# Modulation vectors of a diffusion trunk: from VectorE sums to TensorE matmuls with a narrow stationary operand

## The chip, the cores and the metric

One core of a Trainium2 chip runs the whole program. The metric is the device time of one execution in microseconds (us); the figure for a kernel is the median over its runs. TensorE is called PE here, VectorE DVE, ScalarE ACT, GpSimd POOL and SyncE SP; SP issues nearly all DMAs.

## The reference

Two trunk layers work on 640 tokens (512 latent, 128 context) of width 1024, all in float32. Each layer first makes six modulation vectors of length 1024 from a conditioning vector, and uses them around its mixer and its MLP:

```
mod = silu(cond) @ mod_w[li] + mod_b[li]              # 1024 -> 6 x 1024
sh1, sc1, g1, sh2, sc2, g2 = split(mod, 6)
h = rmsnorm(x, norm_mix_pre[li]) * (1 + sc1) + sh1
y = even_mixer(h, ...) if li == 0 else odd_mixer(h, ...)
x = x + g1 * rmsnorm(y, norm_mix_post[li])
h = rmsnorm(x, norm_mlp_pre[li]) * (1 + sc2) + sh2
x = x + g2 * rmsnorm(relu(h @ mlp_w1[li])**2 @ mlp_w2[li], norm_mlp_post[li])
```

There are two conditioning vectors: `c` for the latent tokens, `c_ctx` for the context tokens. So each modulation matrix (1024 x 6144, 25 MB a layer) is multiplied with two vectors only. Layer 0's mixer is a short gated convolution beside differential attention, layer 1's is neighbourhood attention beside windowed attention.

## The kernel before, in words

**Stages.** `run` opens five phases in turn: `first` (constants, norm and the first weights of layer 0), `mix0` (layer 0's mixer), `wide` (its output projection and MLP), `mix1`, and `wide` again for layer 1. In the trace they begin at about 0, 65, 360, 890 and 1200 us; MLP 0 is the part from about 404 to 890, MLP 1 from about 1254.

**Large matmuls.** They run in float32r with both operands split into a high and a low part, three matmuls per product (`gemm_tok` L232 to L234, `gemm_feat` L243 to L245). Weights come as `raw` tiles (three buffers) by DMA on the SP queue, ACT casts the high part and DVE or POOL subtracts the low one (`unit`, L213 to L218). Results go to PSUM buffers that `mm` hands out: two in the mixers; in a `wide` phase it goes round two `mm` buffers, `po` and, in most of the MLP, four `tp` buffers. In the MLP a block of 1024 hidden features is made in two halves, each by eight `gemm_feat` groups whose relu is L487, and then added to the output by ten `gemm_tok` tiles (L501, L503).

**The first two vectors of layer 0** (shift and scale of the mixer) are summed by PE in stage `first` (`mod_quarter`): the stationary operand is `silu32`, 128 x 32, in which two columns hold silu(c) and silu(c_ctx) and the others are zero. Four matmuls go to the four groups of 32 array columns and write the four 32-partition strips of one PSUM tile (L317); DVE copies it (L320), and two small matmuls with a selection matrix turn the sums into columns (L323).

**The other ten vectors** are summed by DVE, in half vectors of 512 (`mod_slab`): four DMAs of 512 KB from `mod_w` into `mraw` (L339), and for each of eight chunks of 128 rows and each of the two conditions one DVE product with a per-partition scalar, added up in `acc` (L295, L297). Later `mod_sum` splits `acc` into high and low parts (ACT L348; L349 on DVE for layer 0, on POOL for layer 1), sums over the partitions with four PE matmuls with `pick`, a stationary operand of two columns (L352), and copies the row `gr` (L356). Shifts and scales go through DRAM to be laid out as columns (`crow`, `mc`) and end in the tables A and B (`mod_dest`); gates get bias and gain and go to DRAM as rows (`grow`), from which `load_gates` broadcasts them.

**Where this work stands.** `background` takes one half vector from a list. Layer 0's vectors 2, 4 and 3 are called for in `mixer0` and its convolution (six half vectors), layer 0's 5 and layer 1's 1, 2 and 0 in blocks 1 and 2 of MLP 0 (eight), layer 1's 4, 3 and 5 in `mixer1` (six).

**Order.** No order is written out. A planner places every instruction on its engine's queue by priority, which is program order, and by its own estimate of when operands and buffers are ready. `high_priority(-300)` puts what is issued under it 300 places later than it stands, so `background` work yields to the work around it. The queues of the engines, and SP's queue of DMAs, are then run strictly in the planned order. `weave` interleaves two generators, attention steps (`main`) and projection tiles (`fill`).

Of the kernel before, what the change touches and what calls it, by code (L numbers as in the profile page):

```python
# [38 lines left out]
class Trunk:  # L39
    def __init__(self, ctx, tc, I, O):  # L40
        self.tc, self.nc, self.I, self.O = tc, tc.nc, I, O
        pool = lambda name, **k: ctx.enter_context(tc.tile_pool(name=name, **k))
        self.const = pool("const", bufs=1)
        self.stats = pool("stats", bufs=10)
        self.small = pool("small", bufs=8)
        self.wpool = pool("w", bufs=1)
        self.s10 = pool("s10", bufs=10)
        self.shared = pool("shared", bufs=1)
        self.ps = pool("ps", bufs=1, space=PSUM)
        self.dram = pool("scratch", bufs=1, space=DRAM)  # L50
        self.n = self.turn = self.deep = 0
        self.begun = []
# [6 lines left out]
    def slot(self, name, dt=F32, c=640):  # L59
# [7 lines left out]
        "mix0": ({"ln": (1024, 3), "ck0": (512, 1), "v0": (768, 2), "e": (640, 4), "pT": (640, 3), "cb": (642, 1), "yd": (640, 2)}, {"big": (1024, 2)}),  # L67
# [48 lines left out]
    def constants(self):  # L116
# [3 lines left out]
        pick = self.tk("pick", 4)  # L120
        nc.vector.memset(pick, 0.0)
        nc.vector.memset(pick[:, 0:4:3], 1.0)
        self.pick = c.tile([P, 2, 2], F32R, name="pick")
        nc.scalar.copy(self.pick.rearrange("p a b -> p (a b)"), pick)
# [25 lines left out]
        self.silu32 = self.tk("silu32", 256, tag="t2").rearrange("p (k c) -> p k c", k=KC)  # L150
# [19 lines left out]
        self.crow = self.dram.tile([2, 2, 1024], F32, name="crow")  # L170
# [76 lines left out]
    def background(self, jobs, n=1):  # L247

        for job in self.begun:
            job()  # L250
        self.begun = []
# [5 lines left out]
    def weave(self, main, n_main, fill, n_fill):  # L257
# [30 lines left out]

    def mod_acc(self, acc, w, kc, first):

        nc = self.nc
        for c in range(2):
            s = self.silu[:, kc, c:c + 1]
            if first:
                nc.vector.tensor_scalar(acc[:, c, :], w, s, None, ALU.mult)  # L295
            else:
                nc.vector.scalar_tensor_tensor(acc[:, c, :], w, s, acc[:, c, :], ALU.mult, ALU.add)  # L297
# [34 lines left out]
    def mod_slab(self, li, vec, half):  # L332
        nc = self.nc
        mw = self.I["mod_w"][li]
        c0 = vec * 1024 + half * 512
        acc = self.tk("acc").rearrange("p (c n) -> p c n", c=2)
        for u in range(4):
            r = self.tk("mraw").rearrange("p (k n) -> p k n", k=2)
            nc.sync.dma_start(r, mw[u * 256:(u + 1) * 256, c0:c0 + 512].rearrange("(k p) n -> p k n", p=P))  # L339
            for j in range(2):  # L340
                self.mod_acc(acc, r[:, j, :], 2 * u + j, u + j == 0)
        return lambda: self.mod_sum(li, vec, half, acc)

    def mod_sum(self, li, vec, half, acc):

        nc = self.nc
        hl = self.wpool.tile([P, 2, 2, 512], F32R, tag="hl", bufs=4, name=self.nm("hl"))
        nc.scalar.copy(hl[:, 0], acc)  # L348
        (nc.gpsimd if li else nc.vector).tensor_tensor(hl[:, 1], acc, hl[:, 0].bitcast(F32), ALU.subtract)  # L349
        p = self.mm()[:2]  # L350
        for i in range(4):
            nc.tensor.matmul(p, self.pick[:, i % 2, :], hl[:, i // 2, i % 2, :], start=i == 0, stop=i == 3)  # L352
        row = self.tk("gr", 512, tag="t2")[:2]
        w = vec // 3
        if vec % 3 < 2:
            nc.vector.tensor_copy(row, p)  # L356
            d = self.crow[vec % 2, :, half * 512:half * 512 + 512]
            nc.sync.dma_start(d, row)
            cols = self.stats.tile([P, 4, 2], F32, tag="mc", bufs=2, name=self.nm("mc"))
            for c in range(2):  # L360
                nc.sync.dma_start(cols[:, :, c], d[c].rearrange("(k p) -> p k", p=P))
            return self.mod_dest(li, vec, half * 4, cols.rearrange("p k c -> p (k c)"))
        r0 = li * 48 + vec * 8 + half * 4
        bias, gain = (self.tk("gr", 512, tag="t2")[:2] for _ in range(2))
        nc.sync.dma_start(bias, self.I["modb"][r0:r0 + 4, :].rearrange("(o k) n -> o (k n)", o=1).to_broadcast([2, 512]))
        r0 = 61 + (2 * li + w) * 8 + half * 4
        nc.sync.dma_start(gain, self.I["vecs"][r0:r0 + 4, :].rearrange("(o k) n -> o (k n)", o=1).to_broadcast([2, 512]))
        nc.vector.tensor_tensor(row, p, bias, ALU.add)
        nc.vector.scalar_tensor_tensor(row, row, ROOT, gain, ALU.mult, ALU.mult)
        gi = (li * 2 + w) * 2  # L370
        nc.sync.dma_start(self.grow[gi:gi + 2, half * 512:half * 512 + 512], row)
# [101 lines left out]
    def mlp(self, li, H, jobs, after):  # L473
# [3 lines left out]
        for b in range(4):  # L477
            F = self.new_h("f")
            for s in range(2):
                self.deep = DEEP if b < 3 and b + s else 0  # L480
                units = self.slab(I["mlp_w1"][li], 0, ((b * 1024 + s * 512, 512),), lo="dve" if b or s else "pool")
                for c0, n in GROUPS:
                    for m in range(4):
                        p = self.mm()
                        self.gemm_feat(units, m, rhs(0, c0, n), rhs(1, c0, n), p[:, :n])
                        q = self.tk("r", 384, tag="t3")[:, :n]
                        nc.scalar.activation(q, p[:, :n], AF.Relu)  # L487
                        hi = F[0][s][:, m, c0:c0 + n]
# [3 lines left out]
                if b:  # L492
                    self.background(jobs)
            for n in range(2):
                units = self.slab(I["mlp_w2"][li], b * 1024, ((n * 512, 512),))
                for t in range(NT):
                    p = self.mm()
                    ap = lambda part: (lambda kc: F[part][kc // 4][:, kc % 4, t * P:(t + 1) * P])
                    self.gemm_tok(units, ap(0), ap(1), p)
                    if b == 0:  # L500
                        nc.scalar.copy(Y[n][:, t, :], p)  # L501
                    else:
                        nc.vector.tensor_tensor(Y[n][:, t, :], Y[n][:, t, :], p, ALU.add)  # L503
                    if b == 3 and n == 1:
                        after(Y, ss, G, t)
                if b == 3 and n == 0:
                    G = self.load_gates(li * 2 + 1)
                    ss = [self.gate_first(Y[0], t, G) for t in range(NT)]
                elif 0 < b < 3:
                    self.background(jobs)  # L510
            if b == 3:
                assert not jobs and not self.begun
# [169 lines left out]
    def mixer0(self, H, jobs):  # L682
# [4 lines left out]
        for h in range(4):  # L687
            fill, n = (chain(self.qkv_head(H, h + 1, heads), conv), 5) if h < 3 else (conv, 0)
            n += CONV_STEPS[h]
            self.weave(self.diff_attn(heads[h], yB), 6, fill, n)  # L690
            if h < 3:
                self.background(jobs)
# [3 lines left out]
    def conv_branch(self, H, jobs, out):  # L696
# [6 lines left out]
        for which, half in ((2, 0), (2, 1), (1, 0), (1, 1), (0, 0), (0, 1)):  # L703
            self.background(jobs, half)
# [95 lines left out]
    def mixer1(self, H, jobs):  # L800
# [54 lines left out]
        def q_tiles():  # L855
            self.background(jobs)
# [15 lines left out]
        def v_tiles():  # L872
            self.background(jobs)
# [37 lines left out]
        def qk_groups(hc):  # L911
            self.background(jobs)
# [168 lines left out]
    def run(self):  # L1081
        jobs = lambda li, vecs: [lambda v=v, h=h: self.mod_slab(li, v, h) for v in vecs for h in range(2)]
# [3 lines left out]
        todo = jobs(0, (2, 4, 3))  # L1086
# [8 lines left out]
        with self.phase("wide"):  # L1095
            H = self.rest(0, y, Y0, todo, jobs(0, (5,)) + jobs(1, (1, 2, 0)))
            todo = jobs(1, (4, 3, 5))
        with self.phase("mix1"):
            y, Y0 = self.mixer1(H, todo)
        with self.phase("wide"):  # L1100
            self.rest(1, y, Y0, todo, [])

    def rest(self, li, y, Y0, todo, jobs):
# [9 lines left out]
        while todo or self.begun:  # L1113
            self.background(todo)
# [99 lines left out]
```

## Time and profile before

| | |
|---|---|
| Median of 3 runs | 1722.18 us (1720.81 to 1725.09) |
| The profiled execution | 1719.25 us; its span, first to last instruction, 1717.4 us |
| Mean granted PE clock | 0.974 of 2.4 GHz |
| PE busy | 1623.5 us, 95% of the span |
| PE weight loads | 1418.3 us, 83% |
| DVE busy | 926.8 us, 54% |
| ACT busy | 665.9 us, 39% |
| POOL busy | 304.3 us, 18% |
| HBM read | 172.93 MB, 109 GB/s in the mean |

The busy share of PE is modelled from pipelined instructions that overlap, so the distance from the start of one matmul to the next says more than the length of one. The granted clock is the mean of two levels, 1.2 and 2.4 GHz: 0.5 in a stretch is all of it at the lower one. A float32 matmul (not float32r) appears as two records.

### The profile page before, as it was taken

The numbers are of one execution on the slowest core, as the hardware profiler recorded it, in microseconds if no ns is written. First come the engines' busy times: TensorE is split into PE (matmuls) and PEld (weight loads), VectorE is DVE, ScalarE is ACT, GpSimd is POOL, SyncE is SP. The second block draws the span as 40 slices with busy tenths as digits, with TensorE's granted clock in tenths as the row PEclk, the third lists the DMA queues.
The fourth block names the chain that finished last, engine by engine and source line by source line (L and its number), as shares of the span: only waits on it lengthen the run. The fifth ranks groups of instructions, "written<-read, shape, count | busy, mean of one in ns | idle before, by whom it ended". The sixth has DMA issues, their size and how long they took to land. (4 is left out here: it accounts for less than half of the span.)

```text
span 1717.4 us, 23382 instructions
## 1 busy us (share of the span) xinstructions
PE 1623.5 (95%) x9088; PEld 1418.3 (83%) x9088; DVE 926.8 (54%) x1539; ACT 665.9 (39%) x1389; POOL 304.3 (18%) x339
## 2 busy tenths in 40 slices
PE   6889998987999999899997899999989999999998
PEld 4878787876989988789886678898789898898996
DVE  3386768637732758754367845743564143342433
ACT  4543443435333313223344645445464242141331
POOL 1342343134000001100144300431330000000002
PEclk9979898999999999999999999999999999999999
DMA  9334314235431434433144214421453131222222
GB/s 298 88 102 123 89 59 122 93 123 173 150 110 50 147 124 142 153 100 122 56 140 149 93 58 134 130 83 53 151 172 99 50 98 54 94 62 86 77 71 86
DMA packets 140015, 187.38 MB, mean 109 GB/s; under 512 B 32499, under 2 KB 71728, under 8 KB 139904
## 3 DMA queue, kind: packets, MB, share of 16 engines
q1 hardware_dynamic: 139904, 185.89, 34.3%
q8 instruction: 71, 1.16, 0.3%
q14 instruction: 40, 0.33, 0.1%
HBM read 172.93 MB, written 14.50 MB: 109 GB/s over the span
## 5 line engine op out<-in xcount | busy, mean ns | idle before, releaser
L297 DVE SCALAR_TENSOR_TENSOR acc<-mraw,silu,acc 128x512 f32<-128x512 f32 x280 | 216.0, 814 | 62.8 <-DMA mraw<-mod_w 62.5
L216 ACT CAST hl<-raw 128x1024 fp32r<-128x1024 f32 (+2 forms) x184 | 169.7, 930 | 181.9 <-DMA raw<-mlp_w 53.4
L218 DVE TENSOR_TENSOR hl<-raw,hl 128x1024 fp32r<-128x1024 f32 (+2 forms) x138 | 161.0, 1181 | 116.3 <-ACT hl L216 115.2
L243 PE MATMUL mm<-hhi,hl 128*128 128x384 f32 (+1 forms) x652 | 208.6, 321 | 7.8 <-DVE gr L356 5.5
L245 PE MATMUL mm<-hhi,hl 128*128 128x384 f32 (+1 forms) x652 | 205.2, 316 | 1.7 <-DVE hl L218 1.6
L244 PE MATMUL mm<-hlo,hl 128*128 128x384 f32 (+1 forms) x652 | 205.0, 315 | 0.8 <-DVE hlo L406 0.8
L490 DVE TENSOR_TENSOR r<-r 128x256 f32<-128x256 f32 (+1 forms) x128 | 62.0, 488 | 147.8 <-ACT fhi L489 147.7
L243 PEld LDWEIGHTS mm<-hhi,hl 128*128 128x128 f32 x652 | 125.6, 193 | 11.6 <-DVE gr L356 6.4
L245 PEld LDWEIGHTS mm<-hhi,hl 128*128 128x128 f32 x652 | 125.1, 192 | 3.2 <-DVE hl L218 1.9
L244 PEld LDWEIGHTS mm<-hlo,hl 128*128 128x128 f32 x652 | 125.7, 193 | 1.5 <-DVE hlo L406 1.1
L441 POOL TENSOR_TENSOR yacc<-yacc,G 128x512 f32<-128x512 f32 x20 | 28.8, 1453 | 519.0 <-ACT junk L385 501.1
L349 POOL TENSOR_TENSOR hl<-acc,hl 128x1024 fp32r<-128x1024 f32 x12 | 31.9, 2661 | 481.5 <-ACT hl L348 481.5
L233 PE MATMUL tp<-hl,fhi 128*128 128x512 f32 x262 | 104.3, 399 | 5.0 <-DVE hl L218 5.0
L234 PE MATMUL tp<-hl,flo 128*128 128x512 f32 x262 | 103.8, 397 | 0.0
L232 PE MATMUL tp<-hl,fhi 128*128 128x512 f32 x262 | 102.6, 398 | 0.0
L218 POOL TENSOR_TENSOR hl<-raw,hl 128x512 fp32r<-128x512 f32 (+1 forms) x46 | 85.4, 1868 | 66.0 <-ACT hl L216 55.0
L232 PE MATMUL mm<-hl,hhi 128*128 128x384 f32 (+2 forms) x232 | 85.4, 371 | 6.6 <-DVE rb L556 4.6
L234 PE MATMUL mm<-hl,hlo 128*128 128x384 f32 (+2 forms) x232 | 84.0, 363 | 3.2 <-DVE hlo L406 3.2
L243 PE MATMUL tp<-hhi,hl 128*128 128x384 f32 (+1 forms) x276 | 86.3, 314 | 0.0
L244 PE MATMUL tp<-hlo,hl 128*128 128x384 f32 (+1 forms) x276 | 86.3, 314 | 0.0
L233 PE MATMUL mm<-hl,hhi 128*128 128x384 f32 (+2 forms) x232 | 84.4, 364 | 1.6 <-POOL hl L218 1.6
L245 PE MATMUL tp<-hhi,hl 128*128 128x384 f32 (+1 forms) x276 | 85.2, 313 | 0.0
(425 smaller groups left out, 3934.6 us busy)
## 6 DMA issues: line engine op xcount, KB each, us to landing
raw<-mlp_w SPq DMA_DIRECT2D x128, 512.0 KB
mraw<-mod_w SPq DMA_DIRECT2D x80, 512.0 KB
mw<-mod_w SPq DMA_DIRECT2D x8, 1024.0 KB
raw<-w_out SPq DMA_DIRECT2D x16, 512.0 KB
xs<-x SPq DMA_DIRECT2D x15, 512.0 KB
x<-xs SPq DMA_DIRECT2D x15, 512.0 KB
raw<-w_in_even SPq DMA_DIRECT2D x48, 128.0 KB
raw<-w_in_even SPq DMA_DIRECT2D x24, 256.0 KB
```

Of the source, the lines that this page charges most:

```text
L216: nc.scalar.copy(hi, raw)
L218: eng.tensor_tensor(hl[:, 1, :, :width], raw, hi.bitcast(F32), ALU.subtract)
L232: nc.tensor.matmul(out, lhi(kc), hi, start=kc == 0, stop=False)
L233: nc.tensor.matmul(out, lhi(kc), lo, start=False, stop=False)
L234: nc.tensor.matmul(out, llo(kc), hi, start=False, stop=kc == nk - 1)
L243: nc.tensor.matmul(out, hi, rhi(kc), start=kc == 0, stop=False)
L244: nc.tensor.matmul(out, hi, rlo(kc), start=False, stop=False)
L245: nc.tensor.matmul(out, lo, rhi(kc), start=False, stop=kc == KC - 1)
L297: nc.vector.scalar_tensor_tensor(acc[:, c, :], w, s, acc[:, c, :], ALU.mult, ALU.add)
L349: (nc.gpsimd if li else nc.vector).tensor_tensor(hl[:, 1], acc, hl[:, 0].bitcast(F32), ALU.subtract)
L441: self.nc.gpsimd.tensor_tensor(Y0[:, t, :], Y0[:, t, :], G[0 if t < NS else 1][:, 0:512], ALU.mult)
L490: nc.vector.tensor_tensor(q, q, q, ALU.mult)
```

## The change

All ten remaining vectors are now summed by PE, as `mod_quarter` does for the first two. `mod_steps` is a generator; one step takes n chunks of 128 rows of one vector (n = 1 in layer 0's mixer, 2 in the MLPs): it asks for the float32 weights of this step and the next (tiles of 128 x 1024, 512 KB each), multiplies each chunk in four matmuls, one for each group of 32 array columns, with `silu32` as the stationary operand and 256 weight columns streamed, and DVE copies or adds the 128 x 256 result into `mrow`. After the eighth chunk `mod_finish` turns the sums into columns with two small matmuls and finishes them there: shifts and scales without DRAM, gates by a scattered write to `grow`. `mod_acc`, `mod_slab`, `mod_sum`, `pick` and `crow` go.

The calls move too: in mixer 0 `weave` makes one call after each of the 24 attention steps (three vectors, eight steps each); in the MLPs there is a call after every four `gemm_feat` groups and after token tiles 1 and 4. Layer 1's vectors 1, 0, 2, 4 and 3 are all made in MLP 0, after layer 0's 5 (24 steps), and layer 1's 5 at the start of MLP 1 (four steps); mixer 1 has none. The tag `ln`, which holds the weights, gets four buffers instead of three in the wide phases.

```diff
-        "wide": ({"ln": (1024, 3), "G": (1024, 2), "hx": (2048, 1), "t3": (512, 6)}, {"tp": (512, 4)}),
+        "wide": ({"ln": (1024, 4), "mrow": (256, 2), "G": (1024, 2), "hx": (2048, 1), "t3": (512, 6)}, {"tp": (512, 4)}),
...
     def background(self, jobs, n=1):
-        for job in self.begun:
-            job()
-        self.begun = []
         for _ in range(n):
-            if jobs:
-                with self.tc.high_priority(-300):
-                    self.begun.append(jobs.pop(0)())
+            with self.tc.high_priority(-300):
+                next(jobs, None)
...
             next(main)
+            self.background(jobs)
...
+    def mod_steps(self, vecs, n, ahead):
+        nc = self.nc
+        steps = [(li, vec, k) for li, vec in vecs for k in range(0, KC, n)]
+        tiles = {}
+        for i, (li, vec, k) in enumerate(steps):
+            for j in range(i, min(i + ahead + 1, len(steps))):
+                if j not in tiles:
+                    l, v, k0 = steps[j]
+                    tiles[j] = [self.tk("mraw") for _ in range(n)]
+                    for m, w in enumerate(tiles[j]):
+                        r0 = (k0 + m) * P
+                        nc.sync.dma_start(w, self.I["mod_w"][l][r0:r0 + P, v * 1024:v * 1024 + 1024])
+            p = self.mm()[:, :256]
+            for m, w in enumerate(tiles[i]):
+                w = w.rearrange("p (h g n) -> p h g n", h=2, g=4)
+                for g in range(4):
+                    nc.tensor.matmul(p[32 * g:32 * g + 32].rearrange("p (h n) -> p h n", h=2), self.silu32[:, k + m, :],
+                                     w[:, :, g, :], start=m == 0, stop=m == n - 1)
+            if k == 0:
+                rows = self.tk("mrow", 256)
+                nc.vector.tensor_copy(rows, p)
+            else:
+                nc.vector.tensor_tensor(rows, rows, p, ALU.add)
+            if k + n == KC:
+                self.mod_finish(li, vec, rows)
+            yield
+
+    def mod_finish(self, li, vec, rows):
+        nc = self.nc
+        q = self.mm()[:, :16]
+        pick = self.ident.rearrange("p (g r) -> p g r", r=32)[:, :, 0:2]
+        for h in range(2):
+            nc.tensor.matmul(q[:, 8 * h:8 * h + 8].rearrange("p (g c) -> p g c", c=2), rows[:, h * P:(h + 1) * P], pick,
+                             start=h == 0, stop=True, skip_group_check=True)
+        if vec % 3 < 2:
+            return self.mod_dest(li, vec, 0, q)
...
+        nc.vector.tensor_tensor(gate, q.rearrange("p (k c) -> p c k", c=2), b, ALU.add)
+        g = self.npost(li, w).unsqueeze(1).to_broadcast([P, 2, 8])
+        nc.vector.tensor_tensor(gate, gate, g, ALU.mult)
+        for c in range(2):
+            nc.sync.dma_start(self.grow[(li * 2 + w) * 2 + c, :].rearrange("(k p) -> p k", p=P), gate[:, c, :])
...
-        todo = jobs(0, (2, 4, 3))
+        todo = self.mod_steps([(0, 2), (0, 4), (0, 3)], 1, 1)
...
-            H = self.rest(0, y, Y0, todo, jobs(0, (5,)) + jobs(1, (1, 2, 0)))
-            todo = jobs(1, (4, 3, 5))
+            H = self.rest(0, y, Y0, todo, self.mod_steps([(0, 5), (1, 1), (1, 0), (1, 2), (1, 4), (1, 3)], 2, 1))
...
-            self.rest(1, y, Y0, todo, [])
+            self.rest(1, y, Y0, iter(()), self.mod_steps([(1, 5)], 2, 1))
```

## Rows read from the trace of the kernel before

**Rows 1.** By stretch: PE, PEld, DVE, ACT, POOL busy, PE clock, DMA, GB/s:
```profile
80.00:350.00 270.00, 251.37 (x1368) 215.98 (x1367) 198.69 (x343) 114.27 (x280) 85.73 (x95) 0.92 0.32 95
...
880.00:960.00 80.00, 64.96 (x344) 53.34 (x342) 63.12 (x99) 38.31 (x89) 41.20 (x47) 0.93 0.43 139
...
1290.00:1690.00 400.00, 400.00 (x2223) 362.42 (x2222) 143.79 (x201) 123.99 (x195) 6.45 (x5) 1.00 0.23 74
```

**Rows 2.** The same stretches, instructions that touch the tile acc alone:
```profile
80.00:350.00 270.00, 0.00 (x0) 0.00 (x0) 84.74 (x102) 6.29 (x6) 0.00 (x0) 0.92 0.32 95
...
880.00:960.00 80.00, 0.00 (x0) 0.00 (x0) 21.38 (x28) 1.05 (x1) 2.40 (x1) 0.93 0.43 139
```

**Rows 3.** One line's instructions: ns min/median/max, first and last start; relus, picks:
```profile
L487 ACT ACTIVATE r<-mm x12: 364/385/493, 418.3 to 588.1; 128x256 f32<-128x256 f32 x7, 128x384 f32<-128x384 f32 x5
...
L487 ACT ACTIVATE r<-mm x16: 366/491/493, 588.1 to 830.2; 128x384 f32<-128x384 f32 x10, 128x256 f32<-128x256 f32 x6
...
L487 ACT ACTIVATE r<-po x7: 365/387/492, 1266.8 to 1431.9; 128x256 f32<-128x256 f32 x4, 128x384 f32<-128x384 f32 x3
...
L487 ACT ACTIVATE r<-po x9: 383/387/492, 1431.9 to 1654.9; 128x256 f32<-128x256 f32 x5, 128x384 f32<-128x384 f32 x4
...
L352 PE MATMUL mm<-hl,pick x20: 386/394/402, 587.9 to 801.8; 128*2 128x512 f32 x20
```

**Rows 4.** What PE waited for: us in total, times, longest:
```profile
PE mm L243 <- DVE gr L356: 5.5, 2, 4.5
...
PE tp L233 <- DVE hl L218: 5.0, 1, 5.0
...
PE mm L232 <- DVE rb L556: 4.6, 1, 4.6
...
PE s L1061 <- DVE nx L968: 4.2, 3, 3.5
...
PE pt L564 <- DVE e L765: 3.7, 3, 1.8
```

**Rows 5.** Short stretches, columns as in Rows 1:
```profile
85.00:112.00 27.00, 21.41 (x76) 16.15 (x76) 24.99 (x37) 10.54 (x27) 15.51 (x18) 0.63 0.35 110
...
177.00:198.00 21.00, 18.78 (x76) 14.24 (x76) 16.48 (x24) 8.45 (x18) 11.15 (x12) 0.76 0.40 121
...
286.00:294.00 8.00, 6.55 (x28) 6.55 (x29) 8.00 (x15) 0.62 (x1) 6.36 (x4) 0.57 0.54 144
...
928.00:935.00 7.00, 4.63 (x11) 3.70 (x12) 6.84 (x11) 0.00 (x0) 1.66 (x1) 0.52 0.50 151
```

**Rows 6.** PE in order of time, stage first: start us, us, records:
```profile
39.82 1.52 PE L317 MATMUL pt<-mw,silu 128*32 128x256 f32 x12
...
41.27 0.44 PE L676 MATMUL mm<-hl,hhi 128*128 128x384 f32 x1
...
46.57 0.34 PE L678 MATMUL mm<-hl,hlo 128*128 128x384 f32 x1
...
46.74 0.51 PE L678 MATMUL acc<-hl,hlo 128*128 128x384 f32 x2
...
47.18 1.93 PE L317 MATMUL pt<-mw,silu 128*32 128x256 f32 x32
```

**Rows 7.** PE in order of time, the small matmuls of stage first:
```profile
21.90 0.58 PE L323 MATMUL tp<-sel,mr 128*128 128x4 f32 x4 [0.62 <-DVE mr L320]
```

**Rows 8.** PE in order of time, one set of pick matmuls:
```profile
706.83 1.09 PE L352 MATMUL tp<-hl,pick 128*2 128x512 f32 x4
```

**Rows 9.** Two lines of stage first, columns as in Rows 3:
```profile
L317 PE MATMUL pt<-mw,silu x128: 376/380/637, 15.9 to 48.7; 128*32 128x256 f32 x128
...
L320 DVE COPY mr<-pt x4: 418/425/425, 21.3 to 49.2; 128x256 f32<-128x256 f32 x4
```

**Rows 10.** What DVE waited for, columns as in Rows 4:
```profile
DVE acc L297 <- DMA mraw<-mod_w: 62.5, 39, 4.0
```

**Rows 11.** DVE by line, 85 to 112 us: busy us, mean ns, idle before:
```profile
L297 DVE SCALAR_TENSOR_TENSOR acc<-mraw,silu,acc 128x512 f32<-128x512 f32 x16 | 13.4, 886 | 1.0 <-DMA mraw<-mod_w 1.0
```

More of the change, by code (lines that the diff above doesn't have):

```diff
@@ L66 @@
         "first": ({"x0": (1024, 1), "junk": (512, 3), "mw": (2048, 4), "mr": (256, 2), "ab": (8, 8)}, {"acc": (512, 2), "tp": (512, 2)}),
-        "mix0": ({"ln": (1024, 3), "ck0": (512, 1), "v0": (768, 2), "e": (640, 4), "pT": (640, 3), "cb": (642, 1), "yd": (640, 2)}, {"big": (1024, 2)}),
+        "mix0": ({"ln": (1024, 3), "ck0": (512, 1), "v0": (768, 2), "e": (640, 4), "pT": (640, 3), "cb": (642, 1), "yd": (640, 2), "mrow": (256, 1)}, {"big": (1024, 2)}),
         "mix1": ({"ln": (1024, 3), "cvs": (2048, 1), "e": (512, 3), "pT": (512, 2), "mask": (768, 1), "win": (384, 1), "bias": (1024, 2), "ckT": (512, 1)},
                  {"s": (512, 2), "pe": (512, 2)}),
-        "wide": ({"ln": (1024, 3), "G": (1024, 2), "hx": (2048, 1), "t3": (512, 6)}, {"tp": (512, 4)}),
+        "wide": ({"ln": (1024, 4), "mrow": (256, 2), "G": (1024, 2), "hx": (2048, 1), "t3": (512, 6)}, {"tp": (512, 4)}),
     }
@@ L119, in constants @@
         make_identity(nc, self.ident)
[L120 to L124, printed above, removed]
         self.mhalf = c.tile([P, 8], F32, name="mhalf")
@@ L149, in constants @@
                                 e.rearrange("p (c k) -> p c k", c=2), ALU.mult)
-        self.silu32 = self.tk("silu32", 256, tag="t2").rearrange("p (k c) -> p k c", k=KC)
+        self.silu32 = c.tile([P, KC, 32], F32, name="silu32")
         nc.gpsimd.memset(self.silu32.rearrange("p k c -> p (k c)"), 0.0)
@@ L247, in background, with weave @@
     def background(self, jobs, n=1):
-        for job in self.begun:
-            job()
-        self.begun = []
         for _ in range(n):
-            if jobs:
-                with self.tc.high_priority(-300):
-                    self.begun.append(jobs.pop(0)())
-    def weave(self, main, n_main, fill, n_fill):
+            with self.tc.high_priority(-300):
+                next(jobs, None)
+    def weave(self, main, n_main, fill, n_fill, jobs=iter(())):
         done = 0
@@ L287, in mod_dest @@
             nc.vector.tensor_tensor(out, pv, b, ALU.add)
[L289 to L297, printed above, removed]
     def mod_load(self, i):
@@ L330, in mod_quarter @@
         return out
-    def mod_slab(self, li, vec, half):
+    def mod_steps(self, vecs, n, ahead):
         nc = self.nc
[L334 to L342, printed above, removed]
@@ L344, in mod_sum @@
-    def mod_sum(self, li, vec, half, acc):
-        nc = self.nc
[L347 to L353, printed above, removed]
-        w = vec // 3
[L355 to L371, printed above, removed]
@@ new lines, in mod_finish @@
+    def mod_finish(self, li, vec, rows):
+        nc = self.nc
+        q = self.mm()[:, :16]
[5 more added lines that the diff above has]
+            return self.mod_dest(li, vec, 0, q)
+        w = vec // 3
+        gate = self.sm("gate", 16).rearrange("p (c k) -> p c k", c=2)
+        b = self.modb[:, li * 48 + vec * 8:][:, :8].unsqueeze(1).to_broadcast([P, 2, 8])
+        nc.vector.tensor_tensor(gate, q.rearrange("p (k c) -> p c k", c=2), b, ALU.add)
[3 more added lines that the diff above has]
+            nc.sync.dma_start(self.grow[(li * 2 + w) * 2 + c, :].rearrange("(k p) -> p k", p=P), gate[:, c, :])
@@ L505, in mlp @@
                         after(Y, ss, G, t)
+                    elif t % 3 == 1:
+                        self.background(jobs)
                 if b == 3 and n == 0:
@@ L508, in mlp @@
                     ss = [self.gate_first(Y[0], t, G) for t in range(NT)]
[L509 to L512, printed above, removed]
+        assert next(jobs, None) is None
     def w_out(self, li, n, gs, y, sink, lo="dve"):
@@ L689, in mixer0 @@
             n += CONV_STEPS[h]
-            self.weave(self.diff_attn(heads[h], yB), 6, fill, n)
-            if h < 3:
-                self.background(jobs)
+            self.weave(self.diff_attn(heads[h], yB), 6, fill, n, jobs)
         yA, Y0 = out
@@ L703, in conv_branch @@
         for which, half in ((2, 0), (2, 1), (1, 0), (1, 1), (0, 0), (0, 1)):
-            self.background(jobs, half)
             units = self.slab(w, 0, ((which * 512 + half * 256, 256),), lo="pool")
@@ L797, in diff_attn, with mixer1 @@
         yield
-    def mixer1(self, H, jobs):
+    def mixer1(self, H):
         nc, I, O = self.nc, self.I, self.O
@@ L855, in q_tiles @@
         def q_tiles():
-            self.background(jobs)
             units = self.slab(w, 0, ((1536, 512),), lo="pool3")
@@ L872, in v_tiles @@
         def v_tiles():
-            self.background(jobs)
             units = self.slab(w, 0, ((1024, 512),), lo="3pool")
@@ L1081, in run @@
     def run(self):
-        jobs = lambda li, vecs: [lambda v=v, h=h: self.mod_slab(li, v, h) for v in vecs for h in range(2)]
         with self.phase("first"):
@@ L1095, in run @@
         with self.phase("wide"):
-            H = self.rest(0, y, Y0, todo, jobs(0, (5,)) + jobs(1, (1, 2, 0)))
-            todo = jobs(1, (4, 3, 5))
+            H = self.rest(0, y, Y0, todo, self.mod_steps([(0, 5), (1, 1), (1, 0), (1, 2), (1, 4), (1, 3)], 2, 1))
         with self.phase("mix1"):
-            y, Y0 = self.mixer1(H, todo)
+            y, Y0 = self.mixer1(H)
         with self.phase("wide"):
-            self.rest(1, y, Y0, todo, [])
+            self.rest(1, y, Y0, iter(()), self.mod_steps([(1, 5)], 2, 1))
     def rest(self, li, y, Y0, todo, jobs):
@@ L1112, in rest @@
             pass
-        while todo or self.begun:
-            self.background(todo)
+        for _ in todo:
+            pass
         G = self.load_gates(li * 2)
```

3 lines of the change are left out of this document (removed).

## The prediction

> **What bounds the kernel now.** I read the busy time by stage first, then the same stages for the tiles of the old sums alone, then what the TensorE (PE) waited for, then the stretches in which its clock fell. In the second MLP the PE is busy without a gap, 400.0 of 400 us at full clock; in layer 0's mixer it is busy 251.4 of 270 at a granted clock of 0.92, and VectorE (DVE) 198.7 [rows 1]. So a microsecond of PE work added to an MLP costs a microsecond, while in the mixers chains through DVE decide part of the time. The old sums are 84.7 of those 198.7 us, and 21.4 of DVE's 63.1 where layer 1's mixer begins [rows 1, 2].
>
> What they cost the PE can be measured, because the two MLPs do the same work and only the first has modulation beside it. The first half of layer 0's relus, 418.3 to 588.1, takes 169.8 us and layer 1's 165.1; the second half, 588.1 to 830.2, takes 242.1 against 223.0. All eight sets of pick matmuls of this MLP lie in the second half, 587.9 to 801.8 [rows 3]: they and the waits around them cost 19.1 us.
>
> **What goes.** Twenty half slabs, each with 16 DVE products, an ACT cast, a subtraction on DVE or POOL, four pick matmuls, and a trip of the row through DRAM. What DVE loses is by itself worth nothing where the PE is the bound. On the PE a set of four lasts 1.09 us, one of them 0.39 [rows 3, 8], so they start 0.23 apart and a set is worth 0.93: six sets in mixer 0, 5.6 us; eight in MLP 0, 7.5 of the 19.1; six in mixer 1, 5.6.
> Waits of the PE that I hold the old DVE work for: for gr 5.5 us (4.5 of it at 282, in mixer 0), rb 4.6, nx 4.2, e 3.7, and hl 5.0, which is inside the 19.1 [rows 4]. After most of them the clock falls to 1.2 GHz: 0.57 granted over 286 to 294, 0.52 over 928 to 935 (959 to 966 is like it), 0.63 over 85 to 112, 0.76 over 177 to 198 [rows 5]. A stretch loses its length times (1 - granted): 3.4, 3.4 (twice), 10.0 and 5.0 us.
>
> **What comes.** Ten vectors of eight chunks of 128 rows, four matmuls a chunk. The first stage already runs this shape for two other vectors: 32 records (16 matmuls, two records each) in 1.93 us, four column groups side by side [rows 6]. One record lasts 0.38 [rows 9], so the eight rounds are 0.22 apart; a chunk is two rounds, 0.44 us, and ten vectors are 160 rounds, 35 us.
> Each step changes from 128 array columns to 32 and back. Before the 32 records, two L678 take 0.51 where one takes 0.34, so the second starts near 46.91, and the next record at 47.18: 0.27 where the L678 are 0.17 apart, 0.09 or 0.1 in. The twelve records from 39.82 end at 41.34, so their last starts near 40.96, and L676 follows at 41.27: 0.31 instead of 0.22, 0.09 out [rows 6]. I take 0.18 a step for both.
> The Trainium skill (TensorEngine Tiling (Array Packing), Key Properties) says that changing the tiling mode drains the engine, which speaks against 52 small steps. Read as a full drain, a switch would cost the rest of the last matmul's modelled length, 0.16 each way, and the 52 steps 17 us instead of 9.4; the rows show about half of that, and I go by them.
> Finishing a vector is two small matmuls, four records; the like in the first stage take 0.58 [rows 7]; I take 0.6.
> By stage:
> - Mixer 0: 24 steps of one chunk, 24 x (0.44 + 0.18) = 14.9, and three finishes 1.8: 16.7.
> - MLP 0: six vectors in 24 steps of two chunks, 24 x 1.06 = 25.4, and 3.6: 29.0, all on a saturated PE.
> - MLP 1: four steps and a finish, 4.8.
> - Mixer 1: nothing.
>
> **New waits.** A step holds one of the PSUM buffers that the gemms rotate through (two in the mixers) until DVE has copied it, 0.42 us for this shape [rows 9]. The nearest row is the wait for gr, 5.5 us over twenty sets, 0.28 a set; the ends are 0 and mixer 0's own rate, 4.5 us in one set of six, 0.75 a step or 18 us for its 24 steps. DVE was full of the old sums then, so I take 0.17 a step there, 4 us, and 1.7 in the MLPs, where up to seven buffers rotate.
> The PE now waits for the weights itself. DVE waited 62.5 us in 39 turns for them, 1.6 each [rows 10]; if half of the 52 steps did so it would be 42 us. The loads now go out one step ahead, some 14 us in mixer 0 (340 us over 24 steps), and a step has lower priority than the work around it, so I cost this at nothing; that distance hides it, and 42 is the price if it is gone. Behind a waiting matmul stand all gemms; behind a load that waits for its buffer stand the weight loads of the sync queue, as before.
> The added DVE work, a copy or add per step (52 x 0.42 = 22 us) and two or three small ones per vector, lies beside the PE's matmuls. The gates leave in a scattered write instead of a row, and each is read a stage later, or at the end of its own MLP; off the path.
>
> **The sum.**
> - Mixer 0: +16.7 work, -5.6 picks, -7.9 for the wait at 282 with its clock (4.5 + 3.4). Of the rest (clock 10.0 + 5.0, e 3.7, 19 us in all) I take 9: over 85 to 112 the old products are 13.4 of DVE's 25.0 busy us [rows 5, 11], so half of that jam goes, but the ACT and POOL links of the softmax chain stay. The steps fall partly into gaps that are left, -3, and new waits are +4. Together -4.8; the ends are -23 (the whole pool, 7 hidden, no waits) and +21.
> - MLP 0: +29.0 - 19.1 + 1.5 = +11.4; ends +6 and +25.
> - Mixer 1: -5.6 picks; rb 4.6, nx 4.2, the second gr wait 1.0 and two clock falls 6.8 make 16.6, of which I take 13.5, since over 880 to 960 a third of DVE's work was these sums [rows 1, 2]. -19.1; ends -24 and -9.
> - MLP 1: +4.8 + 0.2 = +5.0; ends +3 and +9.
> Together -7.5 us. The profiled execution took 1719.25 us (its span is 1717.4), so 1711.8; the median of the runs, 1722.18, lies 2.9 above it, so the forecast is 1715 us. About 0.3%, 5.2 us, is what a measurement of this kernel can tell from no change: faster is below 1717.0, slower above 1727.3.
>
> **Rivals.**
> - The mixers give more: the steps fill the gaps of mixer 0 and its clock stays up: the other 10 of those 19 us and 2 more hidden. For it: the falls follow waits of a few us that a step could shorten. Against: a step lasts 0.6 us and comes at low priority. 1703.
> - The mixers give less, because ACT or POOL is next late: 4.5 of the 9 in mixer 0, 9.5 of the 13.5 in mixer 1. +8.5, 1723, no change. For it: POOL was busy 15.5 of the 27 us over 85 to 112 too [rows 5]. Against: the products there [rows 11].
> - PSUM turns (the slower side). In mixer 0 a step between two gemms takes the buffer that the second would have had, and it waits for the first one's evacuation. At 1 us a step that is 24 us where I took 4, 1735. It decides from about 0.5 us a step, where the gain is used up. For it: the wait at 282 was of this kind. Against: the planner can put a step where attention work, with other buffers, comes next.
> - The change doesn't do what it says: the column groups run one after another. 160 rounds become 640, 105 us more, 1820. Against: the rounds of rows 6 are four wide in the same shape; only the streamed operand's pattern differs.
>
> **Chances.** Forecast 0.45 (its own range 1707 to 1723), more 0.17, less 0.18, PSUM 0.17, one after another 0.03. Faster: 0.62 of the first, all of the second and a tenth of the third, 0.47; same: 0.36 of the first and 0.7 of the third, 0.29; slower 0.24. Range 1696 to 1735: below it lies a tail of the second, above it half of the fourth and the fifth.
>
> **What would show it.** 640 records on the new line in rounds of four, 0.22 apart. The first half of MLP 0's relus some 14 us longer than now (twelve steps, three finishes), near 184, its second half near 238; MLP 1's first half near 170. No PE wait for gr, rb or nx; a granted clock over 85 to 112 above 0.63. From the last relu of MLP 0 to the first of MLP 1, now 436.6 us [rows 3], some 19 less. Wrong would be: PE waits at the new matmuls for their weights, gemms of mixer 0 that wait for the new copies, or the same gaps in the mixers with another engine named.

## The result: slower, and where the microseconds went

The changed kernel takes 1734.88 us (median of 4 runs, 1734.1 to 1735.66) against 1721.49 for the kernel before beside it: a ratio of 1.0077 (95% interval 1.0061 to 1.0092). Faster was forecast, 1715. The profiled execution took 1735.66 us, its span is 1733.9, so 16.5 more than the span of before.

Five marks cut both spans into the same stages: the last matmul of the first gemm (61.6 us before, 70.5 after), the first and last relu of MLP 0, the first and last relu of MLP 1. The relus of the changed kernel stand on line 473; the columns are those of [rows 3], and for each half of an MLP the rows that hold its first or last relu are shown:

```profile
L473 ACT ACTIVATE r<-tp x16: 383/438/511, 456.4 to 607.3; 128x256 f32<-128x256 f32 x8, 128x384 f32<-128x384 f32 x8
...
L473 ACT ACTIVATE r<-mm x11: 361/418/492, 421.5 to 591.0; 128x256 f32<-128x256 f32 x6, 128x384 f32<-128x384 f32 x5
...
L473 ACT ACTIVATE r<-mm x15: 365/392/492, 702.9 to 864.6; 128x256 f32<-128x256 f32 x8, 128x384 f32<-128x384 f32 x7
...
L473 ACT ACTIVATE r<-mm x13: 365/491/491, 1277.1 to 1443.3; 128x384 f32<-128x384 f32 x8, 128x256 f32<-128x256 f32 x5
...
L473 ACT ACTIVATE r<-po x8: 383/436/491, 1277.6 to 1447.5; 128x256 f32<-128x256 f32 x4, 128x384 f32<-128x384 f32 x4
...
L473 ACT ACTIVATE r<-po x8: 383/385/493, 1514.2 to 1671.1; 128x256 f32<-128x256 f32 x5, 128x384 f32<-128x384 f32 x3
```

MLP 0 begins at 421.5, is half done at 607.3 and ends at 864.6; MLP 1 runs from 1277.1 over 1447.5 to 1671.1.

| Stage | before, us | after, us | difference | forecast | whole steps (second experiment) |
|---|---|---|---|---|---|
| to the end of the first gemm | 61.6 | 70.5 | +8.9 | 0 | +7.9 |
| from there to MLP 0 (mixer 0) | 356.6 | 351.0 | -5.6 | -4.8 | -7.1 |
| MLP 0, first half | 169.8 | 185.8 | +16.0 | +14 | +10.6 |
| MLP 0, second half | 242.1 | 257.3 | +15.2 | -4 | -1.6 |
| from MLP 0 to MLP 1 (mixer 1) | 436.6 | 412.5 | -24.1 | -19.1 | -24.4 |
| MLP 1 and the rest | 450.6 | 456.8 | +6.2 | +5.0 | +3.7 |

Both mixers did what was forecast or better. Two stages did not: MLP 0 grew by 31, not 11.4, and the first stage, which the prediction did not count, by 8.9.

The mixers first, in the changed kernel, by stretch, columns as in [rows 1]:

```profile
80.00:350.00 270.00, 261.69 (x1599) 219.98 (x1600) 123.71 (x259) 111.95 (x280) 76.42 (x110) 0.97 0.32 96
...
85.00:112.00 27.00, 23.50 (x113) 18.40 (x113) 7.10 (x17) 8.01 (x25) 6.23 (x12) 0.82 0.25 81
...
880.00:960.00 80.00, 73.66 (x388) 62.06 (x386) 44.82 (x75) 40.97 (x100) 37.72 (x54) 0.98 0.35 111
```

Over 80 to 350 the PE is busy 261.7 of 270 us at a granted clock of 0.97, where it was 251.4 at 0.92; DVE has 123.7 us of work instead of 198.7. Over 880 to 960 the clock is 0.98 (0.93 before). Over 85 to 112 it is 0.82 (0.63 before [rows 5]), but here the mixer itself begins 9 us later. The first 50 us of the mixer, of the kernel before and of the changed one:

```profile
62.00:112.00 50.00, 40.84 (x185) 34.36 (x185) 31.93 (x49) 20.77 (x56) 32.39 (x48) 0.80 0.25 78
...
71.00:121.00 50.00, 35.11 (x173) 28.43 (x173) 14.97 (x30) 18.31 (x49) 23.56 (x45) 0.80 0.19 61
```

The clock is 0.80 in both: the jam at the beginning has not gone, it comes earlier. The gain lies behind it, where the clock up to MLP 0 is 0.99 (121 to 418 us) instead of 0.95 (112 to 415). What the PE waits for, columns as in [rows 4]:

```profile
PE pt L608 <- POOL qk L543: 11.1, 4, 4.6
...
PE pt L297 <- DMA mw<-mod_w: 5.9, 3, 2.5
...
PE tp L329 <- DMA mraw<-mod_w: 4.2, 3, 1.9
...
PE mm L225 <- DVE rb L540: 0.4, 1, 0.4
```

The waits for gr and nx are gone, rb is 0.4 of 4.6; qk from POOL, 11.1 us between 70 and 86 (0.8 before), is what is late next as the mixer begins. The late modulation loads of the first stage (mw) cost 5.9 (4.3 before), and waits for the new weights have come: 4.2 us in this row, 4.8 with a second one of 0.6.

Now three pieces of MLP 0, PE in order of time (start us, us, engine, line, shape, records):

```profile
691.25 0.33 PE L237 MATMUL tp<-hlo,hl 128*128 128x384 f32 x1
691.52 0.62 PE L329 MATMUL tp<-mraw,silu 128*32 128x256 f32 x2
692.07 0.44 PE L238 MATMUL tp<-hhi,hl 128*128 128x384 f32 x1
692.44 0.62 PE L329 MATMUL tp<-mraw,silu 128*32 128x256 f32 x2
692.99 0.45 PE L236 MATMUL tp<-hhi,hl 128*128 128x384 f32 x1
```

```profile
486.50 0.63 PE L329 MATMUL tp<-mraw,silu 128*32 128x256 f32 x6
487.06 0.50 PE L227 MATMUL po<-hl,flo 128*128 128x512 f32 x1
487.49 0.64 PE L329 MATMUL tp<-mraw,silu 128*32 128x256 f32 x8
489.39 0.62 PE L329 MATMUL tp<-mraw,silu 128*32 128x256 f32 x2 [1.26 <-DMA mraw<-mod_w]
489.94 0.51 PE L225 MATMUL tp<-hx,fhi 128*128 128x512 f32 x1
```

```profile
695.47 1.24 PE L329 MATMUL mm<-mraw,silu 128*32 128x256 f32 x15
697.24 0.61 PE L346 MATMUL po<-ident,mrow 128*128 128x8 f32 x4 [0.54 <-DVE mrow L335]
697.90 0.59 PE L329 MATMUL mm<-mraw,silu 128*32 128x256 f32 x2
```

In the first, two of the new matmuls stand alone between gemm matmuls. Each is two records 0.24 us apart, with one column group of four at work, and the array is changed over to 32 columns and back for it: from 691.25 to 692.07 the PE does one 384-column matmul, which takes 0.17, and one lone matmul. In the second, six records stand apart from eight, and the last two of that step come after 1.26 us of waiting for weights that had not landed. In the third, the four small records that finish a vector stand right behind its last step; the PE waits for DVE's addition (0.54 us) and changes the array over once more. The 384 records of MLP 0's steps form 134 rounds, of which 66 are four wide and 34 hold a single record, where 96 rounds of four had been counted; and the 24 steps, with their finishes, stand in 43 fragments. All told the PE's time around the new matmuls of MLP 0 (start of the matmul before to start of the one behind, less what the one before takes by itself) is 48.8 us; 29.0 was forecast. Idle time does not make the stage longer: the PE is busy 435.8 of the 443.1 us of MLP 0, and was 397.1 of 411.9, so it idles 7.3 us instead of 14.8.

The first stage: SP's queue in order of time, of the changed kernel and of the one before (start us, us, line, transfer):

```profile
27.03 1.00 SPq L285 DMA_DIRECT2D mw<-mod_w  x2
28.13 4.05 SPq L206 DMA_DIRECT2D raw<-w_in_even  x1
32.27 3.89 SPq L285 DMA_DIRECT2D mw<-mod_w  x2
```

```profile
27.03 7.84 SPq L305 DMA_DIRECT2D mw<-mod_w  x4
```

One weight load now stands between the two pairs of late modulation loads. It holds the queue for 4.05 us, so the second pair starts at 32.3 us. In the kernel before, the third load starts at 28.1, holds the queue for 3.98, and the fourth starts at 32.2. So the queue alone moves one load by 4 us. The PE's order was drawn anew too (changed kernel):

```profile
46.73 0.81 PE L297 MATMUL pt<-mw,silu 128*32 128x256 f32 x4
...
51.19 1.50 PE L297 MATMUL pt<-mw,silu 128*32 128x256 f32 x22
...
58.04 0.63 PE L297 MATMUL pt<-mw,silu 128*32 128x256 f32 x6
...
63.42 0.69 PE L660 MATMUL mm<-hl,hhi 128*128 128x384 f32 x1 [3.61 <-ACT hhi L391]
```

The last 32 records of the first stage's own modulation sums, in one piece at 47.18 before [rows 6], are now in three pieces. The last piece stands behind 30 more matmuls of the gemm, and the PE did not wait in front of any of the three. What is made from these sums comes late: the last 30 matmuls of the gemm start at 63.42 after 3.61 us of waiting, and the first of them run at a granted clock of 0.50 (63.4 to 67.5 us).

### The profile page after: what moved, and what is told of

Read it like the earlier page. It is cut to its first block, busy times and chain, and to the rows that moved or that the text cites. A ratio compares the mean times of both kernels' runs of the same rounds, so it can differ in the third digit from the quotient of the medians.

```text
span 1733.9 us, 24106 instructions
## 1 busy us (share of the span) xinstructions
PE 1661.7 (96%) x9688; PEld 1423.4 (82%) x9688; DVE 686.7 (40%) x1232; ACT 645.0 (37%) x1368; POOL 245.6 (14%) x327
## 4 chain that ended last, share of the span: by engine, by line
PE 86%; DMA 4%; issue 3%; POOL 2%; DVE 2%; SPq 1%; ACT 1%; POOLq 0%; DVEq 0%; ACTq 0%
PE mm L225 7%; PE mm L227 7%; PE mm L226 7%; PE mm L236 6%; PE mm L238 6%; PE mm L237 6%; PE tp L225 4%; PE tp L226 4%; PE tp L227 4%; PE tp L236 3%; PE tp L238 3%; PE tp L237 3%; PE po L959 3%; PE po L225 2%; PE po L226 2%
## 5 line engine op out<-in xcount | busy, mean ns | idle before, releaser
L236 PE MATMUL mm<-hhi,hl 128*128 128x256 f32 (+1 forms) x652 | 205.4, 317 | 7.1 <-ACT r L473 5.1
L237 PE MATMUL mm<-hlo,hl 128*128 128x256 f32 (+1 forms) x652 | 203.7, 313 | 2.1 <-DVE hlo L392 2.1
L238 PE MATMUL mm<-hhi,hl 128*128 128x256 f32 (+1 forms) x652 | 204.3, 315 | 0.0
L211 POOL TENSOR_TENSOR hl<-raw,hl 128x512 fp32r<-128x512 f32 (+1 forms) x46 | 74.6, 1635 | 152.5 <-ACT hl L209 139.0
L225 PE MATMUL tp<-hl,fhi 128*128 128x512 f32 x240 | 95.5, 399 | 0.0
L226 PE MATMUL tp<-hl,fhi 128*128 128x512 f32 x240 | 95.0, 397 | 0.0
L227 PE MATMUL tp<-hl,flo 128*128 128x512 f32 x240 | 94.7, 396 | 0.0
L236 PE MATMUL tp<-hhi,hl 128*128 128x256 f32 (+1 forms) x294 | 92.0, 314 | 0.0
L237 PE MATMUL tp<-hlo,hl 128*128 128x256 f32 (+1 forms) x294 | 91.1, 311 | 0.0
L238 PE MATMUL tp<-hhi,hl 128*128 128x256 f32 (+1 forms) x294 | 91.1, 311 | 0.0
L225 PE MATMUL mm<-hl,fhi 128*128 128x512 f32 x186 | 73.8, 397 | 0.0
L226 PE MATMUL mm<-hl,fhi 128*128 128x512 f32 x186 | 73.2, 394 | 0.0
```

Of the source, the lines that this page charges most:

```text
L211: eng.tensor_tensor(hl[:, 1, :, :width], raw, hi.bitcast(F32), ALU.subtract)
L225: nc.tensor.matmul(out, lhi(kc), hi, start=kc == 0, stop=False)
L226: nc.tensor.matmul(out, lhi(kc), lo, start=False, stop=False)
L227: nc.tensor.matmul(out, llo(kc), hi, start=False, stop=kc == nk - 1)
L236: nc.tensor.matmul(out, hi, rhi(kc), start=kc == 0, stop=False)
L237: nc.tensor.matmul(out, hi, rlo(kc), start=False, stop=False)
```

## Experiments

The kernel before ran beside each of them, at a median of 1721.9 to 1722.2 us. Stages are those of the table, read from each profiled execution. Times are medians.

**1. The load order.** The planner orders instructions over the whole first stage, and the five lines that build `pick` stand ahead of it; without them it had drawn the order anew.
```
+        pick = self.tk("pick", 4)
+        nc.vector.memset(pick, 0.0)
+        nc.vector.memset(pick[:, 0:4:3], 1.0)
+        self.pick = c.tile([P, 2, 2], F32R, name="pick")
+        nc.scalar.copy(self.pick.rearrange("p a b -> p (a b)"), pick)
```


> The changed kernel with the five lines that build the old, now unused pick tile put back in the constants; nothing else. They cost nothing by themselves, but the planner then writes the load queue of the first stage in the old order: x, vr, mb, and all four late modulation loads ahead of the fourth pair of weight loads. My theory: the first gemm's last matmul came 9.5 us later (70.1 against 60.6 us) because one weight load was put between those modulation loads and held the queue 4 us for its buffer; then it is back at 60 to 62 here, and the time falls by 6 to 10 us, to about 1727. If the late start is given back in the mixer behind it: the first gemm at 61, the time no more than 2 us lower. If the start varies from run to run or is slowed by the transfers themselves: still near 70, time 1735.

Measured: 1727.51 us, ratio to before 1.0033 (1.0022 to 1.0044). SP's queue:

```profile
27.47 5.53 SPq L290 DMA_DIRECT2D mw<-mod_w  x4
```

And the last sums of the first stage on the PE:

```profile
45.57 1.93 PE L302 MATMUL pt<-mw,silu 128*32 128x256 f32 x32
```

The four late modulation loads stand together again, the 32 records are whole again, and the first gemm ends at 61.6 us, to the tenth as before. The time falls by 7.4 us, and mixer 0 keeps a part (-2.9 instead of -5.6): the late start had been given back in part. MLP 0 is still 28 us longer. So the new order is a second cause, and not the larger one. What in it costs the time was not separated by a run: the held load, the changed place of x, vr and mb in the same queue, or the sums in three pieces. The traces speak for the last. In the three profiles with the new order the sums are cut into 4, 22 and 6 records, the last at 56.6 to 58.0 us, with 3.6 us of waiting for ACT behind; in all others they are whole, at 45.6 to 50.4.

**2. Whole steps.** The loop over a step's matmuls gets a higher priority; its loads, copies and finish keep the low one.
```
-            for m, w in enumerate(tiles[i]):
+            with self.tc.high_priority(600):
+                for m, w in enumerate(tiles[i]):
```


> The changed kernel with the new matmuls alone raised in priority, so that the planner leaves the 4 or 8 matmuls of a step together (52 groups instead of 76 fragments, 18 of them single matmuls). Theory cut up: MLP 0 cost 31.5 us more instead of 11.4 because the steps were cut into fragments, each of which pays the change of array columns and leaves column groups unused; here MLP 0 gives back 15 to 20 us, the time is 1715 to 1720, and the PE time around the new matmuls of MLP 0 falls from 48.8 to about 30. Rival, waits of their own: the excess is waiting for weights, for the row before a finish and for PSUM buffers; it stays, time above 1730. Rival, raised matmuls now stop the gemms for their weights: PE waits at the new line for the DMA of several us, time 1735 or above.

Measured: 1706.53 us, ratio 0.9905 (0.9885 to 0.9925): 28.4 us less than the changed kernel, and faster than the kernel before. A step of MLP 0, PE in order of time:

```profile
600.65 0.39 PE L225 MATMUL tp<-hl,fhi 128*128 128x512 f32 x1
600.97 1.07 PE L330 MATMUL tp<-mraw,silu 128*32 128x256 f32 x16
601.97 0.50 PE L225 MATMUL po<-hl,fhi 128*128 128x512 f32 x1
602.30 0.40 PE L226 MATMUL po<-hl,fhi 128*128 128x512 f32 x1
```

Sixteen records in one piece, and the gemm goes on 1.00 us after its start. All 96 rounds of MLP 0 are four wide, the PE's time around the new matmuls falls from 48.8 to 28.7 us, and the stage from +31.2 to +9.0. The relus, columns as above:

```profile
L474 ACT ACTIVATE r<-tp x16: 383/438/502, 454.2 to 599.5; 128x256 f32<-128x256 f32 x8, 128x384 f32<-128x384 f32 x8
...
L474 ACT ACTIVATE r<-mm x11: 361/415/493, 419.1 to 582.8; 128x256 f32<-128x256 f32 x6, 128x384 f32<-128x384 f32 x5
...
L474 ACT ACTIVATE r<-mm x15: 367/392/492, 677.3 to 840.0; 128x256 f32<-128x256 f32 x8, 128x384 f32<-128x384 f32 x7
```

The first half is 180.4 us (419.1 to 599.5), the second 240.5. The waits for weights went too (0.7 us in all at the new line, 4.8 in the changed kernel). MLP 0 gives back 22.2 us, more than the 15 to 20 expected; 2.5 of the rest lie in the last stage, and why is open. Cutting up was the cause, with the waits inside the cut steps; the rival of waits that stay is out, and so is that of raised matmuls stopping the gemms. Experiment 5 tests it from the other side.

**3. Both.** The five lines of experiment 1 and the raised matmuls of experiment 2 together.

> Both edits together: the old load order of the first stage and the steps left whole. If the two causes are independent, the gains add up: 1734.9 less 8 less 17 is about 1710, under the kernel before by 0.6%. If the start is given back in mixer 0, 1716 to 1718.

Measured: 1705.60 us, ratio 0.9896 (0.9877 to 0.9915), 0.9 us below whole steps alone. That is under the 1710 expected, but the sum of the two gains as measured, 1699, was missed. Its profiled execution is the slowest of its six (1709.05; the fastest 1698.94), with the first gemm's end at 66.4. Experiments 6 and 7 take this up.

**4. What the old sums cost.** The kernel before, which now leaves out all but the first products of each half slab:
```
 def mod_acc(self, acc, w, kc, first):
+    if not first:
+        return
```


> The kernel before with all but the first of the 8 x 2 DVE products of each half slab left out (the sums are then of one chunk only); loads, casts, pick matmuls and rows stay. It prices what the DVE sums cost the PE in each stage. The prediction's pricing: mixer 0 16.9 shorter (7.9 and 9), MLP 0 11.6 (19.1 less the picks), mixer 1 13.5; 42 us in all, 1680. Rival, the softmax chains of ACT and POOL are what the mixers wait for: mixer 0 under 8, mixer 1 under 5, and 1700 or more.

Measured: 1690.96 us, ratio 0.9811 (0.9791 to 0.9832): 31.1 us less, where 42 was expected. In the profiled execution (1683.23 us, the fastest of its five and 7.7 below their median, so its stages may be shorter than usual) mixer 0 is 16.6 shorter, with a first stage 2.6 longer; MLP 0 is 9.4 shorter and mixer 1 12.7. Forecast were 16.9, 11.6 and 13.5. By stretch, columns as in [rows 1]:

```profile
80.00:350.00 270.00, 255.28 (x1423) 220.04 (x1422) 137.22 (x266) 121.69 (x297) 73.95 (x102) 0.95 0.35 107
...
85.00:112.00 27.00, 22.81 (x88) 17.21 (x89) 12.58 (x29) 13.00 (x33) 11.69 (x20) 0.75 0.55 169
...
177.00:198.00 21.00, 18.43 (x83) 13.87 (x81) 12.13 (x23) 9.57 (x24) 9.46 (x12) 0.76 0.58 176
...
286.00:294.00 8.00, 8.00 (x50) 7.22 (x48) 3.96 (x8) 3.24 (x7) 2.60 (x3) 1.00 0.04 7
```

By this one profile the mixers' price was near, though not each piece of it: the fall of the clock at 286 to 294 goes (1.00), over 85 to 112 it is in part cured (0.75), and at 177 to 198 it is as before (0.76). There the changed kernel has 0.92, and 1.00 with the old load order (experiment 1), so something else that the change did counts at that place; what, was not tested.

**5. Steps cut on purpose.** In experiment 3's kernel MLP 0's matmuls are handed out singly inside its gemms, at the gemms' own priority.
```
+            if kc % 4 == 1:
+                next(self.cut, None)
```


> The kernel of the run with both edits, but in MLP 0 the 192 matmuls of the 24 steps are handed out one at a time, two in each gemm of 24, so that most stand alone among 128-column matmuls (planned: 141 lone ones over the program). Theory cut up: a lone matmul costs the PE about 0.68 us, as much as four together (fragments of one matmul took 0.68 and of four 0.64 in MLP 0 of the changed kernel), so MLP 0's new matmuls go from 28 us to about 141 x 0.68 + 51 x 0.16 = 104, and the time rises by some 75 us to 1780. If a fragment's price goes by its matmuls (0.14 each, as in a whole step) and the excess was waiting: MLP 0 up by less than 10 us, time under 1716.

Measured: 1798.60 us, ratio 1.0446 (1.0423 to 1.0468), 93 us more than with whole steps. The PE's time around MLP 0's new matmuls, from its first relu on, is 104.3 us, as expected; the time is 18 us past the expectation. (The very first step, ahead of that relu, waits 8.7 us for its weights, but mixer 0's stage is no longer than in experiment 3.) One lone matmul:

```profile
469.82 0.33 PE L246 MATMUL tp<-hhi,hl 128*128 128x384 f32 x1
470.08 0.62 PE L340 MATMUL tp<-mraw,silu 128*32 128x256 f32 x2
470.63 0.44 PE L244 MATMUL tp<-hhi,hl 128*128 128x384 f32 x1
470.91 0.34 PE L245 MATMUL tp<-hlo,hl 128*128 128x384 f32 x1
471.08 0.34 PE L246 MATMUL tp<-hhi,hl 128*128 128x384 f32 x1
```

From 469.82 to 470.63 lie 0.64 us more than the 0.17 of one matmul, and the next one, at 470.91, is late by another 0.10 that my count around the fragment leaves out: over the 129 fragments more, 13 of those 18 us. MLP 0 is 90.7 us longer than in experiment 3, with 161 fragments where there are 32: 0.70 us for each one more.

**6. Finishes later.** Experiment 3's kernel, with the finish of a vector issued behind the next vector's first step, and a second row buffer in mixer 0.
```
-            if k + n == KC:
-                self.mod_finish(li, vec, rows)
+            if done:
+                self.mod_finish(*done)
+            done = (li, vec, rows) if k + n == KC else None
```


> The kernel with both edits, and the two small matmuls that finish a vector put one step later, when the row has long been added (a second row buffer in mixer 0). Finishes stood 0.9 us behind the last step in the changed kernel and the PE waited for the row; with whole steps a finish takes 0.14 to 0.64. Theory: that wait too came with the cutting, so nothing is left to gain, 1704 to 1707. Rival, the PE still waits at each finish for about 0.9 us: ten finishes, 9 us less, 1697.

Measured: 1702.07 us, ratio 0.9878 (0.9857 to 0.9898), between the two theories; the intervals of this and of experiment 3 overlap, and no stage shows ten waits of 0.9 us gone. (Mixer 0 is 4.8 us shorter and the first half of MLP 0 4.6 longer: the mark between them moved.) The trace of experiment 3 has no wait of the PE for a row (mrow) at all, that of the changed kernel three of 0.5 us: the wait at a finish went with the cutting.

**7. The load order again, in the best kernel.** Experiment 6's kernel without the five lines, and with them:

> Whole steps and late finishes, but with the first stage's load order as the change left it (the five pick lines out again). Alone, putting the old order back gave 7.4 us; beside whole steps it gave 0.9. If the held load costs what it cost alone, this is some 6 us slower than the next run, 1708; if mixer 0 gives the late start back, it is within 2 us of it, 1702 to 1704.

> The kernel with all three edits once more, beside the run with the other load order: 1702 as before, first gemm's last matmul at 61 to 66 us against 69 to 70.

Measured: 1708.49 us, ratio 0.9917 (0.9895 to 0.9939), and 1701.20, ratio 0.9876 (0.9854 to 0.9897). 7.3 us, as much as alone: the first gemm ends at 69.0 and at 62.3. Here the two causes do add up; why experiment 3 gained 0.9 only is open beyond the 5 us by which its profiled start differs from experiment 1's in the same order. The kernel with all three edits is the fastest of those that do the whole work, 1.2% below the kernel before.

**8. Fewer steps in mixer 0.** Experiment 3's kernel with
```
-        todo = self.mod_steps([(0, 2), (0, 4), (0, 3)], 1, 1)
+        todo = self.mod_steps([(0, 2), (0, 4), (0, 3)], 2, 0)
```


> The kernel with both edits, and the 24 steps of mixer 0 made 12 of two chunks each, loaded without a step's lead (three buffers hold no more). If a step costs what the switch of columns and its turn in PSUM cost, 0.29 us beyond its 0.44 a chunk, twelve fewer give 3.5 us, and what other waits they caused: 1700 to 1702. If mixer 0 is bound by its chains, the steps lie beside them: 1705, no change. Rival, without the lead the PE waits for the weights, and the time is 1710 or more.

Measured: 1717.78 us, ratio 0.9972 (0.9957 to 0.9988). The PE's time around the new matmuls in mixer 0 falls from 19.2 to 16.3 us, and the mixer is no shorter (355.7 against 354.1): so the steps do not set its length. Nor does the PE wait long for weights there (0.6 us). The loss is in MLP 0 (433.1 us against 421.5), which this edit does not touch but whose plan it moved. The longest of PE's waits from 414 to 850 us, columns as in [rows 4]:

```profile
PE mm L335 <- DMA mraw<-mod_w: 7.8, 1, 7.8
```

One whole step stood ahead of its weights, 7.8 us with the gemms behind it. That is the price that the prediction named for the loads ("42 is the price if it is gone"), a part of it, and in a stage that the edit leaves as it was; the other 4 us of the loss are open.

## Why the prediction was wrong

- **The step that failed: "MLP 0: six vectors in 24 steps of two chunks, 24 x 1.06 = 25.4".** The size of a whole step was near: 1.19 us in the piece shown of experiment 2 (600.65 to 602.30, less two matmuls of 0.23). What failed is that steps stay whole. The low priority appears in the working only as a cover for the loads ("so I cost this at nothing"). With it the planner put matmuls one by one between those of the gemms, on a PE that had no time to spare, and waits for the weights came as well, 4.8 us where nothing was counted. The excess of 20 us around MLP 0's new matmuls is, in shares worked out from the trace: 38 rounds too many at 0.22, 8.2; waits for weights inside steps, 3.9; the rest, 8, I put down to 11 more fragments with their changes of the array and to the finishes stuck to steps, without a price for each. Undoing it gave 22.2 us in this stage and 28.4 in the time. The sign was in the trace of the kernel before: I took the set of [rows 8], four matmuls in a row at the same low priority, for all of them, but five of the twenty sets stand there in two pairs with gemm matmuls between, this one for instance:

```profile
617.88 0.63 PE L352 MATMUL mm<-hl,pick 128*2 128x512 f32 x2
...
619.27 0.63 PE L352 MATMUL mm<-hl,pick 128*2 128x512 f32 x2
```

- **Not forecast: the first stage, +8.9.** I held the first stage for untouched since no edit of weight stands there. Removing five lines was enough for another order of its loads and of its matmuls; it is worth 7.4 us. The rows to be read for it were not those of the old work removed but, in the changed plan, SP's queue and the PE's order.
- **MLP 0's credit, -19.1,** is borne out: with whole steps the stage is +9.0 against +11.4 forecast, and half of the credit (9.4) goes with the DVE products, so they did hold the PE up there.
- **Mixer 0, -4.8.** Measured -5.6, or -2.9 where the start is as before; that it came near is in part luck. Half of the jam over 85 to 112 was to go. It stayed and came earlier, with POOL's qk as what is late (the rival "ACT or POOL is next late", in this place), and more than forecast came behind it. PSUM turns, the rival on the slow side, gave the right time, 1735, by a mechanism that did not occur: the 8-record steps of mixer 0 cost 0.73 us each when whole, not 1.6. That the time lies just inside the stated range, 1696 to 1735, is luck too.
- **Mixer 1, -19.1.** Measured -24.1. The products' share was right (12.7 against 13.5); what more went (casts, picks, rows) was not taken apart. The end of -24 agrees by luck: its terms, 5.6 and 16.6, make -22.2.
- **MLP 1, +5.0.** Measured +5.9 from its first relu to its last, +3.4 with whole steps.
- **The switch, 0.18 a step.** In and out were read rightly from [rows 6], but the first 128-column matmul behind a step is 0.10 us late as well (0.33 for 0.23 at 601.97), so the switch is about 0.3. The reading from the Trainium skill (TensorEngine Tiling (Array Packing), Key Properties: a change of the tiling mode drains the engine), which I set aside, made it 0.32, an estimate; these rows stand nearer to it. Over 52 steps that is some 6 us.
- **A finish, 0.6.** 0.28 to 0.64 in MLP 0 where steps are whole (three of the six stand in two pieces of 0.14); sized a little high.
- Of the signs named, the waits for gr and nx, MLP 1's first half (170.4) and mixer 1 came as said; the clock over 85 to 112 did too, but only because the jam came before that stretch. "Rounds of four, 0.22 apart" did not, and that was the sign that told. Two signs of being wrong came: waits at the new matmuls for their weights, 4.8 us, and a gap in mixer 0 with another engine named, POOL.

## What to carry to other kernels

Work that pays only when its instructions stand together (column groups side by side, a change of array shape per group) has to be given to the planner as one piece: price it whole, then ask what priority each instruction has and what may be put between them. Read the changed plan's order before the sum is believed. And an edit with no work in a stage can still redraw the order of that stage's loads and matmuls: read both first for a shift that begins before the changed code does.

## What the runs showed of the hardware that was not expected

- A lone 256-column float32 matmul on 32 array columns costs a 128-column gemm 0.64 us and the next matmul 0.10 (experiment 5), nearly what four of them side by side cost when counted alike (0.73 in mixer 0 of experiment 2).
- Profiles with the same load order, each of another kernel, differ in the first stage: its gemm ended at 60.3 to 66.4 us in the six variants of the changed kernel with the old order, and at 69.0 to 70.5 in the three with the new one.
